# A joint pool for retention and the second MLP, with own raw places for attention's later weights and the first MLP's adaLN and up tiles

## The chip, the cores and the metric

The kernel runs on one core of a Trainium2 chip. The metric is the device time of one execution in microseconds (us); three executions of the kernel before took 1850.36, 1853.43 and 1853.51 us, and their median, 1853.43, is the time before.

## The reference

Two layers over 512 latent tokens of width 1024, with 256 context tokens beside them. Layer 0 mixes by neighbourhood attention (8 heads) and spatial gating, layer 1 by bidirectional retention (8 heads); each mixer is followed by a gated MLP with a depthwise convolution of width 3 over the tokens. Shift, scale and gate of every block (adaLN) come from a product of a conditioning vector with `ada_w`. Cut to what matters:

```python
for i in range(2):
    mod_lat = silu(c) @ ada_w[i] + ada_b[i]      # six parts: shift, scale, gate, twice
    mod_ctx = silu(c_ctx) @ ada_w[i] + ada_b[i]
    h = modulate(rmsnorm(x, g[i, 0]), sh1, sc1)  # the same for the context
    y = hybrid(h_ctx, h) if i == 0 else retention(h_ctx, h)
    x = x + g1 * rmsnorm(y, g[i, 1])
    h = modulate(rmsnorm(x, g[i, 2]), sh2, sc2)
    x = x + g2 * rmsnorm(conv_ffn(h), g[i, 3])   # context too, in layer 0 only

def conv_ffn(h):                                 # 1024 -> 2 x 2816 -> 1024
    gate, up = split(dwconv3(h @ w_in, conv_w, conv_b), 2)
    return (silu(gate) * up) @ w_out
```

## The kernel before, in words

`Trunk.build` runs five stages one after the other: spatial gating (`sgu`), attention, the first MLP (`ffn`, l = 0, 768 tokens in 770 columns), retention, and the second MLP (`ffn`, l = 1, 512 tokens). Every instruction is issued through `Lane.call` (line 63), so all rows of the profile name that line, and tiles tell them apart. Buffers come from pools: a tile asked for under a tag takes the tag's next place and waits until the readers of the tile that was there are done. A scheduler sets the order in which each engine's instructions stand; once set, each engine works through its row in order. SP issues the loads, and waits in front of a load for its place to be free; POOL (GpSimd) issues the sums in DRAM that collect the MLP's output.

A weight tile of 128 x 1024 (512 KB) is loaded into a raw place, and `split` (line 99) turns it into a high part, copied by ACT, and a low part, subtracted by DVE. A product of two such pairs takes three matmuls (`mm3`, line 142). Raw places are three under the tag "raw" in the pool "bp", and nearly all loads share them: attention's weights, adaLN tiles, the MLP's weights.

Attention (line 883) goes through four pairs of heads with ten steps each. `project_pair` (line 970) loads and splits a pair's q, k and v weights (tiles wq2r, wq2h, wq2l for the third pair's q, and so on) and makes the projections pq, pk, px, py; at step 9 it is called for the pair two on.

The MLP (line 1794) runs over 22 columns j of the hidden width. For each, `weights(j)` loads a gate tile (f0010r is column 10's in the first MLP) and an up tile (f0110r), and makes from them and their sums seven half-size weights (wa, wb, wc, wd with s and q) for a product scheme with seven products in place of eight (px, py, pz). ACT and DVE gather the products in `pre`, `conv` makes the convolution, the silu and the product (cv, g), and every second column the pieces of the output product (wf) with w_out's tiles (fo09r is column 9's) follow; ACT copies them to yp or ypg, and POOL adds them to yd in DRAM. The up tile has a place of its own ("rawu"), the gate and output tiles share "raw". The first two columns are made without the scheme by `plain`: pf from the first tokens' halves (hb), pf100b and its like from the second half of the tokens (b), with weights wp1 (loaded ahead by `early`), wp01, wp10 and wp11. b comes out of the residual of the stage before: yr, xd and the transposes ht of each token tile, then sa or sb and the block sums.

Beside the first MLP run jobs of adaLN (`ada_half`, line 259): six halves of four tiles each (ar), each tile multiplied and added on DVE in four products (acc), taken in turns that `bg` gives at set places of the loop. Beside attention and retention run jobs that use PE (`ada_packed`).

Retention and the second MLP each have a pool of their own. A pool opened where another was closed takes its memory, so the second MLP opens with placeholder tiles that order its places.

## Time and profile before

| | us |
|---|---|
| median of the three runs | 1853.43 |
| the profiled execution | 1849.05 |
| its span, first to last instruction | 1847.3 |
| PE busy | 1771.2 |
| DVE busy | 1411.9 |
| ACT busy | 1134.7 |
| POOL busy | 314.3 |
| mean granted TensorE clock | 0.987 of full |

PE (TensorE) is the matmul engine, DVE (VectorE) and ACT (ScalarE) the elementwise ones, SP the queue that issues loads. In the profile's rows `out<-in` names the tiles, `x` a count. A row of a timeline gives the start, the duration, the engine, and in brackets the idle time of the engine before the instruction with what ended it. A row of the waits gives who waited for whom, the total, the times and the longest. A row of the windows gives each engine's busy time in that stretch, then PE's granted clock (1.00 is full), the mean share of the 16 DMA engines and GB/s.

By the tiles in the trace attention takes from about 108 to 375, the first MLP from 380 to 905, retention to 1465 and the second MLP to the end.

### The profile page before, as it was taken

Reading aid. Unit: us, or ns where it says so; the run is one execution under the profiler, and the core shown is the slowest. Engines: PE = TensorE matmul, PEld = TensorE weight load, DVE = VectorE, ACT = ScalarE, POOL = GpSimd, SP = SyncE. Lnnn points to the kernel's source line nnn. Section 1 sums busy time; section 2 is a strip of 40 time slices with the busy share of each in tenths; the row PEclk is TensorE's granted clock in tenths of the full one; section 3 lists DMA queues with packets and bytes.
Section 4 is the critical chain, followed back from the end, with each engine's and each line's share of the span. In section 5 each row is a group of like instructions: output and inputs, shape, how many; then the busy total and the mean of one; then the engine's idle time right before and its main releaser. Section 6 shows DMA issues by size and latency. Waiting matters only on the chain. (4 is left out here: it accounts for less than half of the span.)

```text
span 1847.3 us, 29784 instructions
## 1 busy us (share of the span) xinstructions
PE 1771.2 (96%) x11240; PEld 1581.0 (86%) x11240; DVE 1411.9 (76%) x2389; ACT 1134.7 (61%) x2078; POOL 314.3 (17%) x453
## 2 busy tenths in 40 slices
PE   6999999999999899999889999999999899899998
PEld 4887777789989799998789989999998789899996
DVE  4544567579797778778787798888899699888887
ACT  4534567556555465564586677667677476666763
POOL 1111211110223122221110001111110201122221
PEclk9999999999999999999999999999999989999999
DMA  8433332324687778677657434666643235677773
GB/s 310 137 106 97 110 109 70 125 71 148 160 187 151 162 147 178 138 168 158 231 186 224 132 126 128 172 168 166 171 116 122 97 116 148 173 194 175 191 175 103
DMA packets 95488, 279.21 MB, mean 151 GB/s; under 512 B 12528, under 2 KB 14064, under 8 KB 95344
## 3 DMA queue, kind: packets, MB, share of 16 engines
q1 hardware_dynamic: 63568, 217.88, 36.4%
q0 software_dynamic: 31200, 59.31, 19.1%
q8 instruction: 88, 1.44, 0.3%
q14 instruction: 56, 0.46, 0.1%
q10 hardware_dynamic: 576, 0.11, 0.0%
HBM read 208.06 MB, written 52.43 MB: 141 GB/s over the span
## 5 line engine op out<-in xcount | busy, mean ns | idle before, releaser
L63 DVE SCALAR_TENSOR_TENSOR cv<-pre,cw,cv 128x769 f32<-128x769 f32 (+1 forms) x176 | 152.8, 880 | 8.0 <-ACT cv L63 7.4
L63 ACT ACTIVATE cv<-pre,cw 128x770 f32<-128x770 f32 (+1 forms) x88 | 81.0, 922 | 39.7 <-DVE pre L63 38.5
L63 DVE SCALAR_TENSOR_TENSOR acc<-ar,cs,acc 128x512 f32<-128x512 f32 x112 | 81.7, 746 | 26.6 <-DMA ar<-in_adaw 17.2
L63 POOL DMA_DIRECT2D yf<-yp x64 | 55.8, 872 | 260.8 <-ACT yp L63 241.9
L63 ACT ACTIVATE pre<-px 128x256 f32<-128x256 f32 (+2 forms) x160 | 54.2, 366 | 41.4 <-PE px L63 40.5
L63 POOL DMA_DIRECT2D yd<-yp x54 | 46.6, 871 | 191.9 <-ACT yp L63 188.0
L63 ACT COPY yp<-wf 128x512 f32<-128x512 f32 x118 | 67.8, 576 | 17.9 <-PE wf L63 17.7
L63 POOL DMA_DIRECT2D yd<-ypg x54 | 45.3, 864 | 154.3 <-ACT ypg L63 153.8
L63 POOL DMA_DIRECT2D yr<-ryp x40 | 32.7, 828 | 136.6 <-ACT ryp L63 125.3
L63 ACT ACTIVATE g<-cv 128x770 fp32r<-128x770 f32 (+1 forms) x44 | 32.4, 737 | 27.8 <-DVE cv L63 27.7
L63 ACT ACTIVATE pre<-py 128x384 f32<-128x384 f32 (+1 forms) x40 | 17.4, 435 | 46.3 <-DVE cv L63 25.5
L63 PE MATMUL px<-hs,wd 128*128 128x384 f32 x240 | 45.3, 336 | 0.1
L63 PEld LDWEIGHTS px<-hs,wd 128*128 128x128 f32 x240 | 42.3, 188 | 2.0 <-DVE pre L63 0.5
L63 ACT ACTIVATE cv<-cv 128x770 f32<-128x770 f32 (+1 forms) x44 | 32.7, 743 | 14.7 <-DVE cv L63 14.4
L63 DVE TENSOR_TENSOR g<-cv,g 128x770 fp32r<-128x770 f32 (+1 forms) x44 | 36.1, 821 | 7.0 <-ACT g L63 6.7
L63 DVE TENSOR_TENSOR pre<-pre,pz 128x256 f32<-128x256 f32 (+1 forms) x60 | 20.9, 371 | 26.4 <-PE pz L63 26.4
L63 PE MATMUL ad<-ar,c 128*32 128x512 f32 (+1 forms) x320 | 39.4, 529 | 0.1
L63 ACT ACTIVATE sc<-sc,sst 128x512 f32<-128x512 f32 x32 | 23.2, 726 | 24.0 <-DVE sc L63 21.9
L63 DVE TENSOR_TENSOR cv<-cv 128x770 f32<-128x770 f32 (+1 forms) x44 | 36.1, 821 | 1.0
L63 POOL TENSOR_TENSOR tm<-slab,mask 128x256 f32<-128x256 f32 (+1 forms) x32 | 25.6, 828 | 65.9 <-DVE sst L63 65.7
L63 DVE CUSTOM_DVE_ANT_0 sc<-s,tm 128x256 f32<-128x256 f32 x32 | 13.5, 420 | 30.4 <-PE s L63 22.8
L63 PEld LDWEIGHTS px<-hs 128*128 128x128 f32 x240 | 31.4, 193 | 5.9 <-DVE pre L63 4.7
(2998 smaller groups left out, 6876.7 us busy)
## 6 DMA issues: line engine op xcount, KB each, us to landing
ar<-in_adaw SPq DMA_DIRECT2D x96, 512.0 KB, 4.3
yf<-yp POOLq DMA_DIRECT2D x64, 256.0 KB, 4.5
yd<-yp POOLq DMA_DIRECT2D x54, 256.0 KB, 5.2
yd<-ypg POOLq DMA_DIRECT2D x54, 256.0 KB, 4.6
yr<-ryp POOLq DMA_DIRECT2D x40, 256.0 KB, 4.4
fin<-xd SPq DMA_DIRECT2D x10, 512.0 KB, 4.1
xd<-xd SPq DMA_DIRECT2D x8, 512.0 KB, 3.1
xn<-in_x SPq DMA_DIRECT2D x6, 512.0 KB, 4.6
```

Of the source, the lines that this page charges most:

```text
L63: r = f(*p, **k)
```

## The change

Three things are done. In attention the q, k and v weights of the third and fourth pair are loaded into a tile of three raw places (`raws3`, tag "sa"); the third pair's loads are asked for ahead of the loop, the fourth's as each place is read, and the splits stand at steps 4, 6 and 8 of the pair two before, in place of its step 9. In the first MLP a tile `ars` of three places under "sa" holds two adaLN tiles, each loaded one unit before its use, and a spare place that takes the up tile of every odd column from 3; the shared places are left to gate and output weights. Each of these jobs gets one more turn at its start, and columns above 15 one more turn each. And retention and the second MLP share a pool ("rfp"), in which the second MLP's tiles take over tags of retention's; `early(1)` also loads and splits wp01 and wp10 during retention's end. In `plain` the second column's convolution comes after the rest of the block sums.

The diff, with `...` where lines are left out:

```diff
     def phase(self, ctx, name, extra):
-        self.xp = ctx.enter_context(self.tc.tile_pool(name=name, bufs=1))
+        self.xp = self.joint or ctx.enter_context(self.tc.tile_pool(name=name, bufs=1))
...
+    def ada_ring(self, n, items):
...
+        t = self.bp.tile([P, n, 1024], F32, name=f"ars{items[0][0]}{items[0][1]}", tag="sa", bufs=1)
+        self.ars = [t[:, i] for i in range(n - 1)]
+        self.spare = t[:, n - 1]
+        self.units = [(l, half, kp) for l, half in items for kp in range(4)]
+        self.unit_n = 0
+        for x, u in zip(self.ars, self.units):
+            self.load(x, self.ada_unit_src(*u))
...
+    def ada_raw(self):
...
+        i, n = self.unit_n, len(self.ars)
+        self.unit_n += 1
+        if i and i - 1 + n < len(self.units):
+            self.load(self.ars[(i - 1) % n], self.ada_unit_src(*self.units[i - 1 + n]))
+        return self.ars[i % n]
...
     def ada_half(self, l, half, streams, gate=None, away=False, fine=False):
...
+        if l == 0 or half < 4:
+            yield
...
-            raw = self.bp.tile([P, 1024], F32, name=f"ar{l}{half}{kp}", tag="raw", bufs=3)
-            self.load(raw, self.ada_unit_src(l, half, kp))
+            if l == 0 or half < 4:
+                raw = self.ada_raw()
+            else:
+                raw = self.bp.tile([P, 1024], F32, name=f"ar{l}{half}{kp}", tag="raw", bufs=3)
+                self.load(raw, self.ada_unit_src(l, half, kp))
...
-            self.b12 = [
-                [self.xp.tile([P, 2, n], F32R, name=f"b12{l}{x}{m}", tag=f"g{x}", bufs=4 if l else 3) for m in range(2)]
-                for x in range(2)
-            ]
+            if l:
+                both = [self.xp.tile([P, 2, 2, n], F32R, name=f"b12{l}{x}", tag=f"gt{x}", bufs=1) for x in range(2)]
+                self.b12 = [[b[:, m] for m in range(2)] for b in both]
+            else:
+                self.b12 = [
+                    [self.xp.tile([P, 2, n], F32R, name=f"b12{l}{x}{m}", tag=f"g{x}", bufs=3) for m in range(2)]
+                    for x in range(2)
+                ]
...
+            self.raws3 = self.bp.tile([P, 3, 1024], F32, name="raws3", tag="sa", bufs=1)
+            raws = [self.pair_raw(2, k) for k in range(3)]
...
+                if i < n and step in (4,6,8) and j < 2:
+                    k = (4,6,8).index(step)
+                    pairs[j + 2].setdefault("w", []).append(self.pair_unit(j + 2, k, raws.pop(0)))
+                    if j == 0:
+                        raws.append(self.pair_raw(3, k))
...
+    def pair_raw(self, j, i):
+        raw = self.raws3[:, i]
+        self.load(raw, self.a["hyb_qkv"][(4 * i + j) * P : (4 * i + j + 1) * P])
+        return raw
...
+    def pair_unit(self, j, i, raw=None):
+        if raw is None:
+            return self.unit(self.a["hyb_qkv"][(4 * i + j) * P : (4 * i + j + 1) * P], f"w{'qkv'[i]}{j}")
+        hi, lo = self.slot(f"w{'qkv'[i]}{j}")
+        self.split(hi, lo, raw)
+        return hi, lo
...
     def project_pair(self, j, pr):
...
-        w = [self.unit(self.a["hyb_qkv"][(4 * i + j) * P : (4 * i + j + 1) * P], f"w{'qkv'[i]}{j}") for i in range(3)]
+        w = pr["w"] if "w" in pr else [self.pair_unit(j, i) for i in range(3)]
...
         def lat(i):
...
-            cos = rp.tile([P, 512], F32, name="cos", tag="cos")
-            sin = rp.tile([P, 512], F32, name="sin", tag="sin")
+            turns = rp.tile([P, 2, 512], F32, name="turns", tag="turns")
+            cos, sin = turns[:, 0], turns[:, 1]
+            tb = rp.tile([P, 2, 2, 4, 256], F32R, name="rtb", tag="blk")
...
-                self.blk["t", i] = rp.tile([P, 2, 4, 256], F32R, name=f"rt{i}b", tag=f"t{i}")
+                self.blk["t", i] = tb[:, i // 2]
...
             def context(h):
...
-                d["sc"] = rp.tile([P, 2, 256], F32, name=f"cs{h}", tag="cs", bufs=1)
+                d["sc"] = rp.tile([P, 2, 256], F32, name=f"cs{h}", tag="acc0", bufs=1)
...
-            cw = fp.tile([P, 44, 4], F32, name=f"cw{l}", tag="cw")
+            cw = fp.tile([P, 44, 4], F32, name=f"cw{l}", tag="cw" if first else "e0")
...
-            if not first:
-                for tag in ("rawu", "wh5", "wl5", "wh6", "wl6", "pre0", "pre1"):
-                    fp.tile([P, 1024], F32R if tag[0] == "w" else F32, name=f"at{tag}", tag=tag, bufs=1)
...
-            pres = [fp.tile([P, 2, W], F32, name=f"pre{l}{i}", tag=f"pre{i}") for i in range(1 if first else 2)]
+            pres = [fp.tile([P, 2, W], F32, name=f"pre{l}{i}", tag=("pre", "st")[l] + str(i)) for i in range(1 if first else 2)]
...
-            else:
-                for tag in ("cv", "wh4", "wl4"):
-                    fp.tile([P, 1024], F32R if tag[0] == "w" else F32, name=f"at{tag}", tag=tag, bufs=1)
-            ng = 3 if first else 4
+            ng = 3
+            held = {}
...
-                "o": ("y0", "y4", "y2") if first else ("w2", "w5", "w6"),
+                "o": ("y0", "y4", "y2") if first else ("w2", "w6", "w5"),
...
             def slot(kind, name):
...
+                if h == "w6":
+                    return [fp.tile([P, 1024], F32R, name=f"{name}{x}", tag=f"rv{m}", bufs=1) for m, x in enumerate("hl")]
...
             def raw(src, name, up=False):
-                if up:
-                    t = fp.tile([P, 1024], F32, name=f"{name}r", tag="rawu", bufs=1)
+                if up and first and up % 2 == 0 and up > 3:
+                    t = self.spare
+                elif up:
+                    t = fp.tile([P, 1024], F32, name=f"{name}r", tag="rawu" if first else "rg", bufs=1)
...
             def win(j, i):
...
-                return raw(a["ffn_in"][r : r + P], f"f{l}{i}{j}", i == 1)
+                return raw(a["ffn_in"][r : r + P], f"f{l}{i}{j}", i and j + 1)
...
             def conv(j, pre):
-                cv = fp.tile([P, 2, W], F32, name=f"cv{l}{j}", tag="cv", bufs=1)
+                cv = fp.tile([P, 2, W], F32, name=f"cv{l}{j}", tag="cv" if first else "of", bufs=1)
...
+                elif not first:
+                    i = j % 4
+                    if i == 1 and not held:
+                        held["g"] = self.bp.tile([P, 4, 512], F32R, name="gsa", tag="sa", bufs=1)
+                    if i in (1, 2):
+                        g = held["g"][:, 2 * i - 2 : 2 * i]
+                    else:
+                        g = fp.tile([P, 2, 512], F32R, name=f"g{l}{j}", tag="turns" if i == 0 else "gt0", bufs=1)
+                    g = [g[:, 0], g[:, 1]]
...
-                        if (j, i) == (js[0], 0):
-                            u = self.wp
-                            ring["i" if first else "o"] += 1
+                        if (j, i) in self.wps:
+                            u = self.wps[j, i]
+                            if first:
+                                ring["i"] += 1
...
-                            if (j, i) == (js[1], 1):
-                                ring["i"] = 3
-                            u = slot("i" if (j, i) == (js[1], 1) else "o", f"wp{i}{j}")
-                        if u is not self.wp:
+                            ring["o"] = 2
+                            u = slot("o", f"wp{i}{j}")
+                        if (j, i) not in self.wps:
...
+                    if j != js[0]:
+                        steps[1 + j]()
+                        for _ in sums:
+                            pass
...
-                    steps[1 + j]()
-                for _ in sums:
-                    pass
+                    if j == js[0]:
+                        steps[1 + j]()
...
             def w_out(f, kind="o"):
...
             def part():
...
-                    tiles = [fp.tile([P, 2 if first else 4, 512], F32, name=f"yp{l}", tag="yp")]
-                    if first:
+                    tiles = [fp.tile([P, 2, 512], F32, name=f"yp{l}", tag="yp")]
+                    if not first:
+                        tiles.append(fp.tile([P, 2, 512], F32, name="ypt", tag="gt1", bufs=1))
+                    else:
...
+            if first:
+                self.ada_ring(3, [(0, 10), (0, 11), (1, 0), (1, 1), (1, 2), (1, 3)])
...
+                if first and j > 15:
+                    self.bg()
...
-        self.lp = None
+        self.lp = self.joint = None
...
+            self.wps = {(0, 0): self.wp}
+            if l:
+                for j, i, tags in ((0, 1, ("rv0", "rv1")), (1, 0, ("wh4", "wl4"))):
+                    if i:
+                        raw = self.xp.tile([P, 1024], F32, name=f"wp{j}{i}r", tag="rg", bufs=1)
+                    else:
+                        raw = self.bp.tile([P, 1024], F32, name=f"wp{j}{i}r", tag="raw", bufs=3)
+                    r = (44 * l + NF * i + j) * P
+                    self.load(raw, a["ffn_in"][r : r + P])
+                    self.wps[j, i] = [self.xp.tile([P, 1024], F32R, name=f"wp{j}{i}{x}", tag=g, bufs=1) for x, g in zip("hl", tags)]
+                    self.split(*self.wps[j, i], raw)
...
+        with ExitStack() as ctx:
+            self.joint = ctx.enter_context(self.tc.tile_pool(name="rfp", bufs=1))
...
```

24 lines of the change are left out of this document (12 added, 12 removed).

## The prediction

> **What bounds the kernel now.** I read the page's engine shares first, then what PE waits for, then windows, then the timelines of four places. PE is the bound; what a change can win is PE's idle time and the time at a lowered clock.
>
> ```profile
> PE 1771.2 (96%) x11240; PEld 1581.0 (86%) x11240; DVE 1411.9 (76%) x2389; ACT 1134.7 (61%) x2078; POOL 314.3 (17%) x453
> PE wf L63 <- ACT ypg L63: 6.5, 2, 4.6
> PE ht L63 <- DVE sb L63: 4.9, 3, 4.1
> PE px L63 <- ACT pre L63: 3.9, 2, 3.1
> PE pf100b L63 <- ACT b L63: 2.8, 1, 2.8
> PE at L63 <- ACT arow L63: 2.0, 1, 2.0
> PE wf L63 <- ACT yp L63: 1.5, 2, 1.3
> PE pq L63 <- ACT wq2h L63: 1.5, 1, 1.5
> PE pq L63 <- DVE wq2l L63: 1.3, 1, 1.3
> ```
>
> PE idles 1847.3 - 1771.2 = 76.1 us. The waits (total, times, longest) are few and long, and ACT or DVE is named as releaser; the question is what those were waiting for. The windows (after PE, PEld, DVE, ACT and POOL come the granted clock, the DMA share and GB/s) show what a gap costs beyond itself:
>
> ```profile
> 188.00:198.00 10.00, 6.87 (x25) 5.40 (x26) 7.90 (x17) 8.13 (x19) 5.87 (x7) 0.66 0.51 161
> 600.00:610.00 10.00, 9.71 (x51) 8.77 (x49) 7.91 (x14) 3.06 (x6) 1.23 (x2) 1.00 1.01 225
> 610.00:620.00 10.00, 5.70 (x23) 5.12 (x24) 7.24 (x11) 5.46 (x11) 2.64 (x3) 0.83 0.46 81
> 650.00:700.00 50.00, 50.00 (x263) 45.84 (x262) 41.25 (x61) 28.99 (x50) 13.29 (x17) 1.00 0.76 153
> 880.00:890.00 10.00, 6.93 (x33) 6.62 (x32) 7.96 (x11) 6.05 (x13) 0.00 (x0) 0.83 0.40 141
> 1470.00:1480.00 10.00, 5.89 (x42) 5.47 (x42) 6.62 (x12) 5.67 (x15) 3.18 (x5) 0.87 0.15 57
> 1480.00:1490.00 10.00, 6.91 (x39) 6.18 (x38) 9.15 (x15) 7.43 (x14) 0.59 (x1) 0.61 0.51 151
> 1500.00:1550.00 50.00, 49.96 (x363) 46.93 (x362) 49.06 (x79) 37.29 (x67) 0.31 (x1) 1.00 0.34 111
> ```
>
> If the clock is either whole or half, a mean of 0.66 over 10 us is 10 x 0.34 / 0.5 = 6.8 us at half speed; each busy one of them loses half a microsecond. From 650 to 700, in the first MLP, PE lost nothing: the steady state is PE's, and the losses lie in single places.
>
> **Part 1, attention.** The third pair's weights: SP, ACT, PE and DVE in turn.
>
> ```profile
> 180.86 0.33 SPq L63 DMA_DIRECT2D ar<-in_adaw  x1
> 181.28 0.38 SPq L63 DMA_DIRECT2D wq2r<-in_hyb_qkv  x1
> 189.45 1.04 ACT L63 ACTIVATE wq2h<-wq2r 128x1024 fp32r<-128x1024 f32 x1
> 190.55 0.74 PE L63 MATMUL pq<-h0a,wq2h 128*128 128x512 f32 x1 [1.50 <-ACT wq2h L63]
> 192.20 1.21 DVE L63 TENSOR_TENSOR wq2l<-wq2r,wq2h 128x1024 fp32r<-128x1024 f32 x1
> 193.46 0.79 PE L63 MATMUL pq<-h0a,wq2l 128*128 128x512 f32 x1 [1.31 <-DVE wq2l L63]
> ```
>
> The load stands behind an adaLN load in SP's row, and its high and low parts are split only when PE wants them. SP's row here, before:
>
> ```order
> L63 DMA slab_2209<-in_rpb 128x1x256
> L63 DMA ar_1858<-in_adaw 128x1024
> L63 DMA wq2r<-in_hyb_qkv 128x1024
> L63 DMA wk2r<-in_hyb_qkv 128x1024
> L63 DMA wv2r<-in_hyb_qkv 128x1024
> ```
>
> and now (raws is the new place of three tiles; pair 2's loads stand far ahead, these are pair 3's):
>
> ```order
> L63 DMA raws_1208<-in_hyb_qkv 128x1024
> L63 DMA ar_1868<-in_adaw 128x1024
> L63 DMA slab_2214<-in_rpb 128x1x256
> L63 DMA raws_1208<-in_hyb_qkv 128x1024 x2
> L63 DMA ar_1872<-in_adaw 128x1024
> ```
>
> No q, k or v load competes for the three shared places any more, and the splits come at steps 4, 6 and 8. That removes 1.50 + 1.31 = 2.8 us, and the slow clock: of 6.8 us at half speed 1.31 is the second gap itself, so (6.8 - 1.3) / 2 = 2.7 us. Sum **5.5**. The splits (1.04 on ACT, 1.21 on DVE, three times each) are moved, not added, into a stage where both have room (8.13 and 7.90 of 10 even in the worst window). Bounds: 2.7, if something else keeps the clock down, to 5.5. The Trainium skill, "TensorE: Matmul & The Clock Gate", section "What's actually happening", has the clock fall after an idle window of about 3.4 us. Here it fell with no gap above 1.50, so the trace disagrees; by the page part 1 would be worth 2.8 and the sum 2.7 us less, 1835.3.
>
> **Part 2, first MLP.** The longest gap, in SP, DVE, ACT and PE, then the two late ones:
>
> ```profile
> 605.13 0.33 SPq L63 DMA_DIRECT2D ar<-in_adaw  x1
> 606.27 0.33 SPq L63 DMA_DIRECT2D fo09r<-in_ffn_out  x1
> 611.44 0.75 DVE L63 SCALAR_TENSOR_TENSOR acc<-ar,cs,acc 128x512 f32<-128x512 f32 x1 [3.53 <-DMA ar<-in_adaw]
> 612.75 1.03 ACT L63 ACTIVATE cv<-pre,cw 128x770 f32<-128x770 f32 x1 [6.91 <-DVE pre L63]
> 614.30 0.80 PE L63 MATMUL wf<-fo06h,g 128*128 128x512 f32 x1 [4.59 <-ACT ypg L63]
> 850.39 0.75 DVE L63 SCALAR_TENSOR_TENSOR acc<-ar,cs,acc 128x512 f32<-128x512 f32 x1 [2.80 <-DMA ar<-in_adaw]
> 878.03 1.06 ACT L63 ACTIVATE fo019h<-fo019r 128x1024 fp32r<-128x1024 f32 x1 [2.78 <-DMA fo019r<-in_ffn_out]
> ```
>
> An adaLN tile is issued at 605.13 and used at 611.44, 6.3 us later; DVE stands 3.53 us in front of it, the conv's input behind it holds ACT for 6.91, and the ypg copies queued behind that hold PE for 4.59. SP before, around this place:
>
> ```order
> L63 DMA ar_5850<-in_adaw 128x1024
> L63 DMA f0011r<-in_ffn_in 128x1024
> L63 DMA ar_5951<-in_adaw 128x1024
> L63 DMA fo09r<-in_ffn_out 128x1024
> L63 DMA ar_6102<-in_adaw 128x1024
> L63 DMA f0111r<-in_ffn_in 128x1024
> ```
>
> and now (ars is the ring of two adaLN places and the spare one, which takes every second up tile):
>
> ```order
> L63 DMA ars_4179<-in_adaw 128x1024 x2
> L63 DMA f0010r<-in_ffn_in 128x1024
> L63 DMA f0110r<-in_ffn_in 128x1024
> L63 DMA fo08r<-in_ffn_out 128x1024
> L63 DMA f0011r<-in_ffn_in 128x1024
> L63 DMA fo09r<-in_ffn_out 128x1024
> L63 DMA ars_4179<-in_ffn_in 128x1024
> ```
>
> The adaLN load runs a unit ahead (of four products each), and gate and output weights keep the three shared places. What can go: 4.59, 1.97 (arow, behind the 850.39 product), 3.06 (px, behind fo019h) and 1.29 (yp) = 10.9, and half of 3.4 us of slow clock in each of the windows 610 and 880, 1.7 + 1.7: together 14.3. The fo019 and yp gaps wait for output weights, which gain only by freer places; I take half of 3.1 + 1.3 + 1.7 = 6.1 off, so 14.3 - 3.0 = **11.3**; bounds 4 (only the first gap, less its clock) and 14.3. Six further turns of the background job are nothing beside a PE that is full; the same number of products runs either way.
>
> **Part 3, retention into the second MLP.** PE, DVE and SP here:
>
> ```profile
> 1472.80 0.28 PE L63 MATMUL pf<-hb,wp1h 128*128 128x256 f32 x1
> 1474.35 0.28 PE L63 MATMUL pf<-hb,wp1l 128*128 128x256 f32 x1
> 1478.74 1.97 PE L63 MATMUL ht<-ident,yr 128*128 128x128 f32 x8 [4.11 <-DVE sb L63]
> 1483.46 0.55 PE L63 MATMUL pf100b<-b,wp1h 128*128 128x256 f32 x1 [2.75 <-ACT b L63]
> 1477.87 0.49 DVE L63 TENSOR_SCALAR yr<-xd,xd3r 128x512 f32<-128x512 f32 x1 [1.19 <-POOL xd3r L63]
> 1482.18 1.22 DVE L63 TENSOR_TENSOR wp01l<-f101r,wp01h 128x1024 fp32r<-128x1024 f32 x1 [0.34 <-DMA acc<-in_adab_row]
> 1476.07 0.32 SPq L63 DMA_DIRECT2D xd<-xd  x1
> 1479.13 0.42 SPq L63 DMA_DIRECT2D f110r<-in_ffn_in  x1
> ```
>
> The last tile's chain (xd3r on POOL, yr on DVE) frees the transposes at 1478.74, and PE has nothing else, because the next weights load after the last xd store. PE's row before:
>
> ```order
> L63 MATMUL pf_15170<-hb_14872,wp1l 128x256
> L63 MATMUL ht_15245<-ident,yr_14708 128x128 x4
> L63 MATMUL ht_15254<-ident,yr_14708 128x128 x4
> L63 MATMUL pf100b<-b_15263,wp1h 128x256
> L63 MATMUL pf101b<-b_15263,wp01h 128x256
> ```
>
> and now, from the end of the blocks for wp01 and wp10 (24 products each, moved here):
>
> ```order
> L63 MATMUL pf_15166<-hb_14844,wp10l 128x256
> L63 MATMUL pf_15166<-hb_14844,wp10h 128x256 x2
> L63 MATMUL pf_15166<-hb_14844,wp10l 128x256
> L63 MATMUL ht_15191<-ident,yr_14668 128x128 x4
> L63 MATMUL ht_15200<-ident,yr_14668 128x128 x4
> L63 MATMUL pf_15219<-hb_14844,wp11h 128x256 x2
> ```
>
> Between 1472.80 and 1474.35 thirteen such products start: 0.119 us each. 48 take 5.7 us and cover the 4.11 gap, the transposes starting 1.6 later; 24 of wp11 behind them take 2.9 and cover the 2.75. The clock: 10 x (0.13 + 0.39) / 0.5 = 10.4 us at half, some 4.0 of them idle (1.2 before 1478.74, 2.75), so 6.4 / 2 = 3.2. PE gets 4.1 + 2.75 + 3.2 = 10.0 us ahead. But from 1500 to 1550 DVE is busy 49.06 of 50; it feeds PE's weights, and itself gains only two splits moved forward into its idle time, 2 x 1.22, a third partly, and the microsecond it idles there: 2.4 to 5, I take 5 less 1 for wp01's split (1.04 and 1.22), which now stands in ACT's and DVE's rows within the first tile's residual chain: **4**; bounds 2 - 2.3 (nothing kept, the splits all on the chain) and 10.0. In SP's row cw, fo10r, wp01r and f111r now stand ahead of the xd stores; wp01r waits for the last rg transposes and f111r for wp01's split, both ahead of the first store's data, so I cost that at nothing beyond the microsecond above. Merging the pools adds and removes no instruction. It moves one load at the start of retention:
>
> ```profile
> 890.95 0.33 SPq L63 DMA_DIRECT2D rcv00r<-in_ret_vg  x1
> 898.32 0.33 SPq L63 DMA_DIRECT2D rcv01r<-in_ret_vg  x1
> ```
>
> rcv00r now waits behind the nine fin loads that stood between these two, at most 898.32 - 890.95 = 7.4 us later. The row after it already lives with such a start, so I cost it at nothing; a context value product that had to wait for all of it would cost up to those 7.4.
>
> **Sum.** 1849.05 (the profiled execution; span 1847.3) - 5.5 - 11.3 - 4 = 1828.2. That execution lies 4.4 under the median 1853.43, so 1853.4 - 20.8 = **1832.6**.
>
> **Rivals.**
> - *DVE keeps all of part 3* (12%): it is 98% busy where PE gets ahead; part 3 gives nothing, 1836.6. Against: DVE idles 0.34 to 1.19 at a time ahead of 1483.
> - *The loads stay late in the first MLP* (14%): the window 600 to 610 shows a DMA share of 1.01, so a load issued earlier meets the output accumulations of POOL; part 2 gives 3, 1840.9. Against: 0.76 in the steady stretch where PE is full. The Trainium skill ("DMA: Bandwidth & Descriptors", "Issuing engines are not separate DMA queues") says that loads of all queues share the same engines, which speaks for this rival; the 1.01 agrees.
> - *SP's row holds gate loads back* (9%), slower: an ars load waits in SP for the products of the unit before, and f0010r or f0012r stand behind it. With 22 such loads, more than 20.8 / 22 = 0.95 us lost at each eats all gains; at 1.5 each, half of the 3.06 behind fo019h, it is 33 - 20.8 = 12 slower, 1865. For: PE gaps behind late fo loads. Against: 650 to 700 has the same loads in the same queue without loss.
> - *It doesn't do what it says* (5%): if the places of one tile are waited for as a whole, or the same gaps come elsewhere, 1853, no difference.
>
> **Numbers.** The forecast has 60%. All gains at their upper bounds are 5.5 + 14.3 + 10.0 = 29.8, 1823.6; at their lower ends 2.7 + 4 + 0 = 6.7, 1846.7. The range 1822 to 1846 holds the forecast and the first two rivals. Faster by over 0.2% (3.7 us, about what a measurement here can tell from none): 0.60 + 0.12 + 0.14 = 0.86; within: 0.05; slower: 0.09.
>
> **Right or wrong.** Right: no PE wait for wq2 and a clock near 1 from 188 on; no DVE idle on adaLN tiles in the first MLP and no 4.59 gap; ht waits under 1 us at the start of the second MLP, with DVE full after it. Wrong: PE waits on wa or fo weights in the first MLP (the SP rival), or on wc and fo splits around 1490 to 1520 that sum to 10 us (the DVE rival).

## The result and the profile after

| | before | changed |
|---|---|---|
| median of four runs, us | 1851.89 | 1834.84 |
| lowest to highest, us | 1848.15 to 1853.51 | 1830.70 to 1836.59 |
| ratio, changed to before | | 0.9918 [0.9891, 0.9944] |
| the profiled execution, us | 1849.05 | 1836.59 |
| its span, us | 1847.3 | 1834.8 |

The changed kernel is faster by 0.82%: 1851.89 x (1 - 0.9918) = 15.2 us, and by the ends of the interval 10.4 to 20.2. The forecast was 1832.6, with 20.8 saved. The profiled execution of the changed kernel is the slowest of its four, so it shows 12.5 of the gain. Two executions below, one of only_mlp1 and one of only_joint, ran at a mean granted clock of 0.845 and 0.890 (1931.92 and 1893.92 us) and are in no ratio, and the profiled execution of ngr_act ran at 0.952 and is in no comparison of stages.

The page's engine shares and the waits of PE in the changed kernel that the argument turns on (who waits for whom, total, times, longest):

```profile
PE 1768.0 (96%) x11240; PEld 1577.6 (86%) x11240; DVE 1410.8 (77%) x2389; ACT 1141.8 (62%) x2084; POOL 315.4 (17%) x453
PE ht L63 <- DVE xn L63: 11.7, 4, 9.3
PE px L63 <- DVE pre L63: 5.0, 4, 1.6
PE wf L63 <- DVE fo05l L63: 3.1, 1, 3.1
PE ht L63 <- DVE yr L63: 3.0, 1, 3.0
PE wf L63 <- ACT ypg L63: 2.6, 2, 2.1
PE s L63 <- POOL kb L63: 2.6, 1, 2.6
PE rx L63 <- DVE of L63: 2.4, 1, 2.4
PE ht L63 <- DVE sb L63: 0.8, 2, 0.4
```

All eight waits shown of before are gone or cut: pq on wq2h and wq2l, pf100b on b, at on arow and wf on yp have no row any more, wf on ypg fell from 6.5 to 2.6, ht on sb from 4.9 to 0.8, px on ACT's pre from 3.9 to 2.3 (shown with tap_after below). But other waits stand there now: s on kb, ht on yr and wf on fo05l, 2.6 to 3.1 us each, and rx on of, which is 2.4 in this execution, 0.65 to 1.76 in the other kernels with the joint pool and 0.91 in the kernel before. The largest of all, ht on xn, lies at the start of the program (11.3 before) and none of the parts bears on it; the next, px on DVE's pre (3.4 before), lies for the most part in the second MLP (3.0 of 5.0). The windows of the changed kernel, laid where the work of the windows shown before now is (the stages start 3 to 15 us earlier), and three more, at 145, 520 and 530:

```profile
145.00:155.00 10.00, 7.41 (x29) 5.87 (x28) 2.62 (x7) 3.42 (x5) 2.00 (x3) 0.83 0.52 193
188.00:198.00 10.00, 9.97 (x59) 6.76 (x59) 6.14 (x20) 7.45 (x21) 4.49 (x6) 1.00 0.49 148
520.00:530.00 10.00, 8.62 (x46) 7.83 (x45) 6.89 (x12) 6.03 (x9) 0.86 (x1) 1.00 0.77 178
530.00:540.00 10.00, 8.32 (x35) 7.39 (x36) 9.97 (x15) 5.70 (x10) 1.72 (x3) 0.83 0.72 158
610.00:620.00 10.00, 10.00 (x45) 8.98 (x44) 10.00 (x15) 5.56 (x12) 3.73 (x5) 0.85 0.96 254
870.00:880.00 10.00, 10.00 (x59) 9.92 (x58) 9.86 (x15) 6.12 (x10) 0.00 (x0) 1.00 0.14 52
1459.00:1469.00 10.00, 10.00 (x79) 9.58 (x78) 8.19 (x13) 6.89 (x16) 2.96 (x4) 1.00 0.31 106
1469.00:1479.00 10.00, 10.00 (x85) 9.79 (x84) 9.18 (x18) 8.22 (x19) 0.00 (x0) 1.00 0.00 0
1489.00:1539.00 50.00, 46.90 (x315) 41.60 (x315) 47.65 (x75) 33.05 (x59) 1.83 (x2) 1.00 0.37 114
```

The window at 188 went from 0.66 of the clock to 1.00, the ones at the joint of retention and second MLP from 5.89 and 6.91 of 10 to full, the one at 880 (now 870) from 6.93 to full. The one at 610 went from 5.70 to full, but its clock is still 0.85 behind a gap of 2.06 that ends at 609.49. The losses moved: 145 to 155 (before, PE was 9.92 busy there at a clock of 1.00), 520 to 540, and the first 50 us of steady work in the second MLP, where PE went from 49.96 to 46.90.

Three rows of PE stand in every kernel here and cut the span into four stages: the first product with the second tokens' b in the first MLP, the first Ykq of retention, and the first kn behind a gap. In the kernel before:

```profile
391.35 0.44 PE L63 MATMUL pf000b<-b,wp0h 128*128 128x384 f32 x1 [1.76 <-ACT b L63]
1081.27 0.50 PE L63 MATMUL Ykq<-h1c,rkq21h 128*128 128x256 f32 x2 [0.95 <-ACT qp L63]
1402.59 1.08 PE L63 MATMUL kn<-ident,kp 128*128 128x128 f32 x4 [2.41 <-DVE kp L63]
```

and in the changed one:

```profile
388.02 0.69 PE L63 MATMUL pf000b<-b,wp0h 128*128 128x384 f32 x1 [1.76 <-ACT b L63]
1066.72 0.50 PE L63 MATMUL Ykq<-h1c,rkq21h 128*128 128x256 f32 x2 [0.96 <-ACT qp L63]
1388.10 1.09 PE L63 MATMUL kn<-ident,kp 128*128 128x128 f32 x4 [2.41 <-DVE kp L63]
```

Stage A (to the first row, with attention) is 391.4 before and 388.0 after; stage B (first MLP and retention's start) 689.9 and 678.7; stage C 321.3 and 321.4; stage D (retention's end and second MLP) 444.7 and 446.7. So in this pair of executions attention gave 3.4, the first MLP 11.2, and the joint with the second MLP took 2.0. Single executions of the same code differ in A and D by 5 to 6 us, as the table of all kernels below shows, so it takes more of them to say what each part gave.

### The profile page after: what moved, and what is told of

Read it like the earlier page. It is cut to its first block, busy times and chain, and to the rows that moved or that the text cites. A ratio compares the mean times of both kernels' runs of the same rounds, so it can differ in the third digit from the quotient of the medians.

```text
span 1834.8 us, 29748 instructions
## 1 busy us (share of the span) xinstructions
PE 1768.0 (96%) x11240; PEld 1577.6 (86%) x11240; DVE 1410.8 (77%) x2389; ACT 1141.8 (62%) x2084; POOL 315.4 (17%) x453
## 3 DMA queue, kind: packets, MB, share of 16 engines
q0 software_dynamic: 31200, 59.31, 19.1%
## 5 line engine op out<-in xcount | busy, mean ns | idle before, releaser
L63 DVE SCALAR_TENSOR_TENSOR acc<-ars,cs,acc 128x512 f32<-128x512 f32 x96 | 70.1, 749 | 19.1 <-DMA acc<-in_adab_row 9.8
L63 ACT COPY yp<-wf 128x512 f32<-128x512 f32 x86 | 49.5, 577 | 13.1 <-PE wf L63 13.1
L63 POOL DMA_DIRECT2D yf<-yp x32 | 28.0, 876 | 160.7 <-ACT yp L63 96.0
L63 POOL DMA_DIRECT2D yf<-ypt x32 | 27.9, 873 | 100.1 <-ACT ypt L63 74.1
L63 PE MATMUL px<-hs 128*128 128x256 f32 x240 | 32.6, 285 | 5.3 <-DVE pre L63 5.0
```

The source lines that it names most:

```text
L63: r = f(*p, **k)
```

## The experiments

The theory after the result was that the three parts add up, each in its own stage, and that what was given back has three places: a bias load in attention, the adaLN places in the first MLP, and DVE behind the joint. The rivals were that a part only works together with another, and that one of the three gives nothing or costs time. Every kernel was timed in five rounds against the kernel before on the same chip.

| kernel | us | before on that chip | ratio |
|---|---|---|---|
| only_att | 1842.24 | 1850.62 | 0.9949 [0.9931, 0.9967] |
| only_mlp1 | 1844.41 | 1850.62 | 0.9964 [0.9948, 0.9981] |
| only_joint | 1848.92 | 1850.62 | 0.9979 [0.9963, 0.9995] |
| again (the changed kernel) | 1833.34 | 1850.62 | 0.9897 [0.9879, 0.9916] |
| ring3 | 1839.15 | 1848.22 | 0.9948 [0.9929, 0.9967] |
| nospare | 1849.74 | 1848.22 | 1.0006 [0.9989, 1.0022] |
| late_split | 1833.34 | 1848.22 | 0.9913 [0.9895, 0.9932] |
| slab2 | 1832.85 | 1848.22 | 0.9922 [0.9900, 0.9944] |
| spare_only | 1840.25 | 1848.19 | 0.9951 [0.9933, 0.9970] |
| wp01_out | 1832.93 | 1848.19 | 0.9907 [0.9879, 0.9936] |
| tap_after | 1821.55 | 1848.19 | 0.9847 [0.9821, 0.9873] |
| ngr_act | 1832.68 | 1848.19 | 0.9917 [0.9887, 0.9946] |

The stages of the profiled executions, and the two new gaps of PE: the one in front of the score product that reads kb (attention) and the one in front of fo05l (first MLP).

| kernel | A | B | C | D | gap kb | gap fo05l |
|---|---|---|---|---|---|---|
| before | 391.4 | 689.9 | 321.3 | 444.7 | none | 0.37 |
| changed | 388.0 | 678.7 | 321.4 | 446.7 | 2.59 | 3.06 |
| again | 387.4 | 681.2 | 321.3 | 443.8 | 2.61 | 3.89 |
| only_att | 385.9 | 685.1 | 321.3 | 448.9 | 1.16 | 0.31 |
| only_mlp1 | 392.0 | 682.9 | 321.4 | 446.3 | 0.89 | 6.55 |
| only_joint | 392.0 | 690.6 | 321.9 | 442.5 | none | none |
| ring3 | 386.2 | 688.1 | 321.4 | 442.4 | 1.47 | 4.29 |
| nospare | 385.1 | 698.7 | 321.2 | 444.3 | 1.91 | 4.31 |
| late_split | 383.0 | 679.1 | 321.5 | 448.0 | none | 3.35 |
| slab2 | 383.2 | 678.8 | 321.4 | 442.1 | none | 3.35 |
| spare_only | 384.9 | 689.1 | 321.6 | 444.8 | 1.85 | 5.91 |
| wp01_out | 386.7 | 682.0 | 321.2 | 442.2 | 1.82 | 4.45 |
| tap_after | 384.7 | 679.9 | 321.4 | 433.7 | 1.12 | 2.56 |

The stages of ngr_act are left out for its clock.

### The parts one by one

**only_att**: the kernel before with the attention part alone. The core of the edit:

```diff
+            self.raws3 = self.bp.tile([P, 3, 1024], F32, name="raws3", tag="sa", bufs=1)
+            raws = [self.pair_raw(2, k) for k in range(3)]
...
+                if i < n and step in (4,6,8) and j < 2:
+                    k = (4,6,8).index(step)
+                    pairs[j + 2].setdefault("w", []).append(self.pair_unit(j + 2, k, raws.pop(0)))
```

> The kernel before with the attention part alone. My theory (each part gives its own share of the sum, 5.5 + 11.3 + 4): 5.5 us faster, no PE wait for wq2 and a full clock around 190. The rival read from the changed kernel's trace (a wait of PE for kb, behind a bias slab's load of 6 us in SP's row, takes the place of the wq2 waits): 3 us faster or less, with a PE gap of some 2.6 us near 145 and 3.4 us at half clock behind it.

Measured: 0.9949 [0.9931, 0.9967], 9.4 us (6.1 to 12.8).

**only_mlp1**: the kernel before with the ring of two adaLN places, the spare up place and the further turns alone.

```diff
+            if first:
+                self.ada_ring(3, [(0, 10), (0, 11), (1, 0), (1, 1), (1, 2), (1, 3)])
...
+                if first and j > 15:
+                    self.bg()
```

> The kernel before with the first MLP's part alone (adaLN ring, spare up place, more turns). My theory: 11.3 us faster, the 4.59 gap gone. The rival (loads still meet the output accumulations): DVE still idles 3 us on an adaLN tile once or twice, 9 us faster. The rival of SP's row, held-back gate loads: slower, or under 4 us faster.

Measured: 0.9964 [0.9948, 0.9981], 6.6 us (3.5 to 9.6).

**only_joint**: the kernel before with the joint pool, wp01 and wp10 early, and the order of `plain` alone (the order in both MLPs).

```diff
+                for j, i, tags in ((0, 1, ("rv0", "rv1")), (1, 0, ("wh4", "wl4"))):
...
+                    self.split(*self.wps[j, i], raw)
```

> The kernel before with the joint pool alone (early wp01 and wp10, the second column's convolution after the block sums in both MLPs). My theory: 4 us faster, the gaps of 4.11 and 2.75 gone. The rival (wp01's split in the residual chain and DVE in the second MLP give the gain back, as the changed kernel's profile has it): no difference or up to 2 us slower, with a gap of about 3 us in front of the second tile's ht transposes and 4 to 6 us more of small PE gaps from 1490 to 1750.

Measured: 0.9979 [0.9963, 0.9995], 3.9 us (0.9 to 6.8).

**again**: the changed kernel, no edit.

> The changed kernel once more, on the same chip as its three parts. If the parts are independent, its difference is the sum of theirs within 3 us (my theory: 20.8, measured first 17). If a part only works with another, the sum is off by more than that.

Measured: 0.9897 [0.9879, 0.9916], 19.1 us (15.5 to 22.4). The product of the three parts is 0.9949 x 0.9964 x 0.9979 = 0.9892, 20.0 us. So within the intervals the parts add up, no part costs time, and none of them needs another.

The stages say the same with other weights. A is 391.8 in the mean of the three kernels without part 1 and 385.8 in the nine that have it and one place for the bias slab (slab2 has two): -6.0. B is 688.5 without part 2 (before, only_att, only_joint) and 680.4 with all of it (seven kernels): -8.1. D is 446.6 without part 3 (before, only_att, only_mlp1) and 444.3 with it (the eight that leave no work out): -2.3, with a spread of 442 to 448. Together 16.4. Between parts 1 and 2 the two ways differ by 3.4 and 1.5, and that is as far as it is settled: only_att's stage B is 4.8 shorter than before's and its D 4.2 longer, though the edit touches neither, so a stage of one execution is good to some 4 or 5 us. One source of that spread is the clock: the executions called changed, again and late_split (whose edit changed nothing, see below) are of one program, and in D, ahead of the last product, the clock fell to half 3, 1 and 4 times for 3.41 us each, up to 1.7 us of work lost each time, and D took 446.7, 443.8 and 448.0.

### The first MLP: which of its two places works

**ring3**: the changed kernel with a third adaLN place in the place of the spare up place.

```diff
-        self.ars = [t[:, i] for i in range(n - 1)]
+        self.ars = [t[:, i] for i in range(n)]
...
-                if up and first and up % 2 == 0 and up > 3:
-                    t = self.spare
-                elif up:
+                if up:
```

> The changed kernel with three adaLN places in the ring and the up tiles back in their single place (the spare is the third). Theory from the last runs (in the changed kernel a load of the ring can start only when the unit before last is read, and where DVE's row has units close together that is some 5 us ahead, as long as a load takes): no DVE wait on ars in the first MLP, the gap of 3 to 6.5 us in front of fo05l's product gone, 2 to 5 us faster than the changed kernel, some 22 under before. Rival (the spare place for the up tiles gives the gain): the adaLN wait goes, but gaps behind up tiles come back, 3 us or more slower than the changed kernel.

Measured: 0.9948 [0.9929, 0.9967]; stage B 688.1. It is slower than the changed kernel, as the rival had it; DVE's waits on adaLN tiles fell to 3.4 and did not go.

**nospare**: the changed kernel without the spare up place and with two adaLN places.

```diff
-                if up and first and up % 2 == 0 and up > 3:
-                    t = self.spare
-                elif up:
+                if up:
```

> The changed kernel with the ring of two adaLN places, and the up tiles back in their single place. If the spare is worth nothing: as the changed kernel, 17 to 19 under before. If the spare carries part 2: 3 us or more slower than the changed kernel, with PE waits on wb or wd behind an up load.

Measured: 1.0006 [0.9989, 1.0022]; stage B 698.7. It loses not 3 us but all of the gain.

**spare_only**: the changed kernel with the spare up place, but with the adaLN tiles back in the three shared places.

```diff
-                raw = self.ada_raw()
...
+            raw = self.bp.tile([P, 1024], F32, name=f"ar{l}{half}{kp}", tag="raw", bufs=3)
+            self.load(raw, self.ada_unit_src(l, half, kp))
```

> The changed kernel with the adaLN tiles back in the three shared places, each loaded when its turn comes; the spare place for every second up tile and the additional turns stay. Theory from the last runs (the spare place carries part 2; the ring's loads are late too where the second stream's accumulator starts late): as the changed kernel, 17 to 19 under before, with DVE waits on adaLN tiles of about 17 in all again. My first theory (the adaLN ring carries part 2): 5 or more slower than the changed kernel.

Measured: 0.9951 [0.9933, 0.9970]; stage B 689.1. The theory that the spare place carries part 2 fell. Parts 1 and 3 alone would make 0.9949 x 0.9979 = 0.9928, and ring3 and spare_only stand at 0.9948 and 0.9951: neither place gains anything by itself, and B goes back to the 688.5 of kernels without part 2. Only both together take it to 680.4. With neither spare nor third adaLN place (nospare) B is 10 longer than without part 2: the ring then costs time. Between the MLP's last product and the first Ykq, where the scheduler set another order for PE, it takes 147.5, against 144.9 in the mean of the three without part 2; the other 7.6 lie in the MLP itself. Why is open. Nor do these kernels differ from the changed one by a place alone: the scheduler gave DVE's row another order in each of them, from 418 on in ring3 and nospare and from 489 on in spare_only.

What DVE waits for in the first MLP shows the one half of the reason. In the kernel before (window 385 to 905), in the changed kernel (380 to 895), and in spare_only (380 to 895):

```profile
DVE pre L63 <- PE pz L63: 15.7, 8, 5.0
DVE acc L63 <- DMA ar<-in_adaw: 12.9, 6, 3.5
```

```profile
DVE pre L63 <- PE pz L63: 40.2, 10, 6.7
DVE acc L63 <- DMA ars<-in_adaw: 9.0, 3, 4.0
```

```profile
DVE acc L63 <- DMA ar<-in_adaw: 19.6, 8, 6.4
```

The ring halves the adaLN waits beside the shared places (9.0 against 19.6 with the same jobs and turns), but it doesn't end them: three remain, up to 4.0. The spare up place shows in the other row: with it DVE stands 40.2 in front of PE's pz (38.6 in spare_only), without it 15.7 before, 13.7 in ring3 and 16.8 in nospare. So with the spare place DVE runs further ahead of PE. What the ring adds shows in PE's rows. Without the adaLN ring the wait of px on pre comes back in spare_only, where the kernel before had 3.06 of it:

```profile
876.95 1.01 PE L63 MATMUL px<-hs,wc21h 128*128 128x384 f32 x2 [3.05 <-ACT pre L63]
```

### The new gap at fo05l

In every kernel with the further turns of the jobs PE waits 2.6 to 6.6 us for the low part of an output weight, which took 0.37 before. In the changed kernel SP, DVE and PE have:

```profile
512.16 0.33 SPq L63 DMA_DIRECT2D f018r<-in_ffn_in  x1
520.78 2.38 SPq L63 DMA_DIRECT2D ars<-in_adaw  x2
```

```profile
525.88 1.42 DVE L63 SCALAR_TENSOR_TENSOR acc<-ars,cs,acc 128x512 f32<-128x512 f32 x2 [3.07 <-DMA ars<-in_adaw]
530.41 1.22 DVE L63 TENSOR_TENSOR fo05l<-fo05r,fo05h 128x1024 fp32r<-128x1024 f32 x1
531.68 0.80 PE L63 MATMUL wf<-fo05l,g 128*128 128x512 f32 x1 [3.06 <-DVE fo05l L63]
```

SP's loads stand still from 512.16 to 520.78, then two adaLN tiles are issued within 2.4, DVE needs the first at 525.88, 5.1 later, and waits 3.07 for it with the split of fo05l behind. PE waits the same 3.06. The weight itself had landed: PE was using fo05h from 528.22 on, so this is DVE's row and no load of an output weight.

The adaLN load is asked for late: SP issues it when DVE has read the place before (520.77), and with the further turns DVE is ready for the next unit 2 us after that, at 522.8; in the kernel before, the load issued at 521.16 was first read at 528.21. Why the place comes free late was followed in the order of the rows: the second stream's accumulator of this half is filled behind the half before's norm rows, for which DVE waits 1.96 (510.84) and 1.26 (514.92), and both streams read each tile. And the load is slow: over its 5.1 us the DMA share is 0.95, which the mean of 0.77 over 520 to 530 hides, and from 520 to 527 the queue that POOL's output sums go by took the larger part of the DMA engines' time, that of the loads 40.0%:

```profile
q0 software_dynamic: 311, 0.57, 57.7%
```

In the other kernels with this gap the tile took from 4.5 us (late_split, gap 3.35) to 7.9 (only_mlp1, gap 6.55) from its issue to DVE's use. Spare_only, which has no ring, has the gap too (5.91, the tile 7.0 after its issue). So the ring neither makes it nor takes it away.

**ngr_act** puts the loads of these norm rows on ACT's queue, where POOL issued them, and gives the bias slab two places (as slab2 does).

```diff
-                G.dma_start(ngr, self.a["norm_g"][row : row + 1, h * 512 : h * 512 + 512].broadcast_to([P, 512]))
+                (S if away else G).dma_start(
+                    ngr, self.a["norm_g"][row : row + 1, h * 512 : h * 512 + 512].broadcast_to([P, 512])
+                )
```

> The changed kernel with two bias slab places, and with the norm weights' row for the first MLP's gate loaded from ACT's queue, not POOL's, where it stands behind accumulations. Theory: DVE's wait for that row (2.6) shrinks below 1, the second stream's accumulator starts earlier, the ring's loads go out earlier, and the gap in front of fo05l's product (3 to 6.5) falls under 2 with its half clock gone; with the slab's 2.6 + 1.7 gone too, 5 to 9 us faster than the changed kernel, 1825 to 1829. Rival (the load is late because of the shared DMA engines): the gap of 3 or more stays; 0 to 4 faster.

Measured: 0.9917 [0.9887, 0.9946]; the gap at fo05l was still 2.70, as the rival had it. The first steps of the theory came about: DVE's wait for the second norm row is gone (that for the first is 2.51), the second stream's first product stands at 513.81 (517.27 in the changed kernel), and the adaLN load goes out at 518.32 (520.78). But DVE has the tile only at 524.93, 1.0 earlier: it took 6.6 us in place of 5.1, at a DMA share of 1.02 (and with PE at 0.95 of its clock). Nor did a third adaLN place close the gap (ring3: 4.29). So its immediate cause is shown by the rows, DVE held by an adaLN tile that lands late; late issue and slow load both have a part in it, and no run separates them.

### Attention: the bias slab

**slab2**: the changed kernel with two places for the bias slab of attention.

```diff
-        slab = ap.tile([P, 256], F32, name=f"slab{h}", tag="slab", bufs=1)
+        slab = ap.tile([P, 256], F32, name=f"slab{h}", tag="slab", bufs=2)
```

> The changed kernel with two places for the bias slab instead of one. Theory (the slab load, which waits for POOL to be done with the slab before and then takes 6 us, holds kb and with it PE at 145): the gap of 2.6 there is gone and the clock full, 2.6 + 1.7 = 4.3 us faster than the changed kernel. Rival (kb waits in POOL's row for something else): no difference.

Measured: 0.9922 [0.9900, 0.9944]; stage A 383.2, no gap at kb. In the kernel before, POOL and PE have here:

```profile
145.65 0.40 POOL L63 TENSOR_SCALAR slab<-slab 128x256 f32<-128x256 f32 x1 [4.63 <-DMA slab<-in_rpb]
146.12 1.59 POOL L63 CAST kb<-kb 64x768 fp32r<-64x768 f32 x2
146.99 0.39 PE L63 MATMUL s<-kb,q 128*128 128x256 f32 x1
```

in the changed kernel SP, POOL and PE:

```profile
140.74 0.62 SPq L63 DMA_DIRECT2D slab<-in_rpb  x1
146.78 0.41 POOL L63 TENSOR_SCALAR slab<-slab 128x256 f32<-128x256 f32 x1 [6.07 <-DMA slab<-in_rpb]
148.13 0.39 PE L63 MATMUL s<-kb,q 128*128 128x256 f32 x1 [2.59 <-POOL kb L63]
```

and in slab2 the window that was at 7.41 and 0.83:

```profile
145.00:155.00 10.00, 10.00 (x64) 8.08 (x62) 5.04 (x15) 6.07 (x11) 0.83 (x1) 1.00 0.51 178
```

POOL stands in front of the slab, whose load waits for its one place, the casts of kb stand behind that on POOL, and PE takes kb as soon as the first cast is done. In the kernel before that was just in time: PE came to kb at 146.9. In the changed kernel PE comes there at 145.53, 1.4 earlier, and the slab took 1.4 longer to land. So the gap is a wait that had no slack before; it shows when PE is ahead, and in only_mlp1, whose attention is as before, it shows with 0.89. A second place takes it away: A is 383.2 (and 383.0 in late_split, where the load took 4.5 us and there was no gap either), against 384.7 to 388.0 where the gap was 1.12 to 2.61. Of the eight executions of part 1 with the gap only three show a fall of the clock behind it (changed, again and wp01_out, A 386.7 to 388.0); the other five have A 384.7 to 386.2. In the whole kernel's time these 2 to 5 us don't show: 0.9922 against 0.9918 and 0.9897 for the changed kernel, within each other's intervals.

### The joint: what was given back

**late_split**: the changed kernel with wp01's split written in `plain`, behind the residual, its load still early.

```diff
+                            if not first and i:
+                                self.split(*u, self.wpr)
...
-                    self.split(*self.wps[j, i], raw)
+                    if i:
+                        self.wpr = raw
```

> The changed kernel with wp01 loaded ahead but split only in the second MLP's first part, after the residual chain. My theory (the split of 1.05 on ACT and 1.22 on DVE stands in the first tile's residual chain): the gap of 2.9 in front of the second tile's ht transposes is 1.5 again, as before, and no half clock follows it; 1 to 3 us faster unless PE then waits for wp01. Rival (the load itself, or DVE's order, makes the gap): it stays 2.9.

Measured: 0.9913 [0.9895, 0.9932]. The edit did nothing: the scheduler put wp01h and wp01l at the same place of ACT's and DVE's rows, in the first tile's residual chain. So it tells nothing on the split and is one more run of the changed program: PE, DVE, ACT and POOL have the same instructions in the same order.

**wp01_out**: wp01's load and split are left out and its products take wp1's tiles.

```diff
-                for j, i, tags in ((0, 1, ("rv0", "rv1")), (1, 0, ("wh4", "wl4"))):
+                self.wps[0, 1] = self.wp
+                for j, i, tags in ((1, 0, ("wh4", "wl4")),):
```

> The changed kernel without wp01's load and split: its products take wp1's tiles instead, the same number of matmuls. My theory (the split stands in the residual chain): the gap in front of the second tile's ht transposes falls from 2.9 to 1.5, the half clock behind it goes, and the chain from gt7l to the second tile's yr takes 15.2 again instead of 17.0; 1 to 3 us faster than the changed kernel. Rival (PE's row, with the transposes moved ahead of two products, makes the gap): it stays near 2.9.

Measured: 0.9907 [0.9879, 0.9936]; stage D 442.2. The changed kernel, on DVE, POOL and PE:

```profile
1437.43 1.22 DVE L63 TENSOR_TENSOR wp01l<-wp01r,wp01h 128x1024 fp32r<-128x1024 f32 x1
1437.63 1.72 POOL L63 TENSOR_SCALAR wyd<-ssyd 128x1 f32<-128x1 f32 x1 [12.59 <-ACT jyd L63]
1449.89 1.54 PE L63 MATMUL ht<-ident,yr 128*128 128x128 f32 x6 [2.95 <-DVE yr L63]
```

and wp01_out:

```profile
1435.58 0.30 POOL L63 TENSOR_SCALAR wyd<-ssyd 128x1 f32<-128x1 f32 x1 [11.07 <-ACT jyd L63]
1446.63 0.98 PE L63 MATMUL ht<-ident,yr 128*128 128x128 f32 x7 [1.45 <-DVE yr L63]
```

With the split the chain from the last low part of the products' input (gt7l) to the second tile's yr takes 1432.33 to 1449.35, 17.0 us; without it 1430.92 to 1446.09, 15.2, which is also what it takes in the kernel before (1443.79 to 1458.96). So the split costs 1.8 in the chain and the 1.5 by which the gap in front of ht grew (1.45 to 2.95). Behind the longer gap the clock is at half for 3.4 us (0.83 in the window 1449 to 1459), 1.7 more; in wp01_out it isn't, but neither is it in the repeat, which has the same gap (2.94). Of the 1.8, 1.4 lie in a step of POOL that took 1.72 in place of 0.30 and overlaps with DVE's making of wp01l; it took 1.71 or 1.72 in all nine kernels with that split there and 0.30 in the three without. In the whole time these 1.5 to 3.2 don't show.

**tap_after**: the changed kernel without one tap of the convolution (w2's product and sum on DVE) in the second MLP.

```diff
-                    V.scalar_tensor_tensor(
-                        out=d[:, 0 : W - 1], in0=s[:, 1:W], scalar=w2, in1=d[:, 0 : W - 1], op0=ALU.mult, op1=ALU.add
-                    )
+                    if first:
+                        V.scalar_tensor_tensor(
+                            out=d[:, 0 : W - 1], in0=s[:, 1:W], scalar=w2, in1=d[:, 0 : W - 1], op0=ALU.mult, op1=ALU.add
+                        )
```

> The changed kernel with one of the convolution's two DVE products left out in the second MLP (the tap of the next token), which takes some 0.6 us a piece and 44 pieces from DVE there. If DVE bounds PE from 1490 on (my theory): the PE gaps behind DVE between 1490 and 1660, 11 to 12 us in the changed kernel, fall under 4, and the kernel is 6 to 10 us faster than the changed one. Rival (late loads make these gaps): they stay above 8, and it is at most 3 faster.

Measured: 0.9847 [0.9821, 0.9873]; stage D 433.7 against 444.3. PE's waits in the second MLP, in the changed kernel from 1485 to 1640:

```profile
PE px L63 <- DVE pre L63: 3.0, 2, 1.6
PE px L63 <- ACT pre L63: 2.3, 2, 1.2
PE px L63 <- DVE wa3l L63: 1.5, 1, 1.5
PE wf L63 <- DVE fo17l L63: 1.0, 1, 1.0
PE wf L63 <- DVE fo13l L63: 0.8, 1, 0.8
PE wf L63 <- DVE fo11l L63: 0.6, 1, 0.6
```

in tap_after from 1480 to 1635:

```profile
PE px L63 <- DVE pre L63: 3.4, 1, 3.4
PE px L63 <- ACT pre L63: 0.4, 1, 0.4
PE wf L63 <- DVE fo11l L63: 0.2, 1, 0.2
```

and in the kernel before from 1490 to 1650:

```profile
PE px L63 <- DVE pre L63: 2.8, 2, 2.6
PE wf L63 <- DVE fo15l L63: 1.3, 1, 1.3
PE px L63 <- ACT pre L63: 0.9, 1, 0.9
```

They sum to 9.2, 4.0 and 5.0. So PE starts the steady part earlier and waits 4.2 more for DVE and ACT in it; with less to do on DVE these waits fall by 5.2 and the stage is 10.6 shorter. DVE's load sets a part of this stage. How much of the 10.6 the kernel before would gain by the same edit wasn't tried.

One row more splits stage D into what the joint gained and what it gave back: the first px of the second MLP, which has the same number of products ahead of it and behind it in every kernel. From the start of D to that row it is 103.5 us in the mean of the three kernels without part 3 and 95.3 in that of the eight with it, 8.2 less; from there to the end 343.2 and 349.1, 5.9 more, and 340.6 in tap_after.

## Why the prediction was right, and where its sizes were off

**The sum.** Forecast 20.8, measured 15.2 (10.4 to 20.2) and, in the repeat, 19.1 (15.5 to 22.4). The sign and the mechanism of each part held; two of the three terms were mis-sized, in opposite directions by the ratios (9.4 for 5.5, 6.6 for 11.3). That the sum came out as near as it did is in part luck.

**Part 1 (term 5.5): right, with a wait it didn't name.** The gaps at wq2 and the slow clock from 188 on are gone, as named. It measured 6.0 by stage A and 9.4 (6.1 to 12.8) by the ratio, all of which lies above the term's upper bound of 5.5; what the ratio has beyond stage A isn't found in any row. The Trainium skill's rule in "TensorE: Matmul & The Clock Gate", section "What's actually happening", by which the slow clock there would not have come from the two short gaps, made it 2.8; the window 188 to 198 at 1.00 without those gaps decides for the trace. What the part gave back is the gap at kb: the step missed is to ask, of the wait that is next on PE's path, how much slack it had. The rows of before show none (kb cast from 146.12, taken at 146.99).

**Part 2 (term 11.3): mechanism right, mis-sized, 6.6 by the ratio and 8.1 by stage B.** The step that failed is "the adaLN load runs a unit ahead": in most turns it does, but at three of the five changes from one half to the next (waits at 526, 791 and 859) it doesn't: at the first of them the two places are released 2.1 us apart and the first load is due by then, so DVE still stands 9.0 in front of adaLN tiles (12.9 before) and the sign "no DVE idle on adaLN tiles" was wrong. That costs the gap at fo05l, 3.06, and the 3.4 at half clock behind it in this execution (0.83 over 10 us is 10 x 0.17 / 0.5), 1.7: 4.8 together. Of the 4.59 gap 2.06 stayed, and the half clock behind it too (from 609.67, 3.4 us), 1.7: 3.8 that the term had counted as gone. The 14.3 of its upper bound less 4.8 and 3.8 is 5.7, near the 6.6 by the ratio. What it removed outright are the gaps of 3.06 (px), 1.97 and 1.29 and the slow clock at 880. The doubt about the output weights, for which 3.0 was taken off, was unneeded, since their gap closed; that it stood in for a part of the 8.6 that came back elsewhere was luck. And the term gave all of the credit to the adaLN places, while ring3 shows that the spare up place is needed as much.

**Part 3 (term 4): right within what can be measured, 3.9 (0.9 to 6.8) by the ratio, 2.3 by stage D.** PE got its full windows (4.11 and 2.75 both closed and the clock at 1.00) and came to the first px 8.2 us earlier, where the forecast had 10.0 ahead of the split; 5.9 of that were given back behind it, 4.2 of them as waits for DVE and ACT. Two signs were wrong in size: ht waits 2.95 and not under 1, since the split in the chain was costed as 1 and costs 1.5 there, with the clock up to 3.2; and the waits on wc and fo splits, named for the rival at 10, sum to 9.2 of all kinds, of which 5.0 stood there before.

**The rivals.** "The loads stay late in the first MLP" is half true: an adaLN load is late, by the order of releases and also by DMA load (a share of 0.95 over its 5.1 us, with POOL's sums as the larger part, against 0.76 in the stretch where PE lost nothing), as this rival had it; but part 2 gave more than the 3 it left (6.6, 3.5 to 9.6). "SP's row holds gate loads back" did not happen in the changed kernel: PE has no wait on a gate weight in the first MLP. Its wait on fo05l is by the letter the sign that was named for this rival, but the weight had landed, and it is DVE's. nospare, which has a wait on a gate weight's split (wa21l, 1.7) and is 10 us longer in B than without part 2, shows that such a loss is near. "DVE keeps all of part 3" fell, narrowly: the part alone is 0.9979 [0.9963, 0.9995], and most of the 8.2 us went back behind it. "It doesn't do what it says" fell with each part's own gain.

## What to carry to other kernels

Where one engine is busy 96% of the time, list its few long waits, find for each the place in memory that the releaser's load was waiting for, and give that load a place of its own; look at what is next on the path and how much slack it has, since a gain of a few microseconds uncovers it. A prefetch ring only runs ahead as long as its places are released in turn: look at the ends of the jobs, where all of them can come free late and close together, and at what else the DMA engines carry just then, over the length of the load and not over a wide window. Try each new place alone, since here two places in one stage gained nothing by themselves and 7 to 8 us together.

## What the runs showed of the hardware that was not expected

PE's clock fell to half behind gaps that are shorter than the 3.41 us for which it then stays there, but not behind every one. In thirteen of the executions (all but ngr_act's) the falls begin whole multiples of 3.413 us apart, in the changed kernel at 148.87, 531.16, 609.67 and 1449.35 among others, and last one, two or three such steps. By the busy times of the traces what decides is how much of one step PE idled: every step with PE idle for more than 0.55 of it was followed by one at half, and from the full clock no fall followed a step idle for less than 0.47. The gap of 3.06 at fo05l lay mostly in one step (PE busy for 0.88 of 3.42), and a fall followed. The gap of 3.35 in late_split lay across two (busy for 1.82 and 1.65 of 3.41 each), and none did. So a gap's length doesn't give its price: the gaps at fo05l, of 2.6 to 6.6, were followed by no fall (late_split, slab2), one step (changed, tap_after) or two (again, only_mlp1, ring3, nospare, wp01_out), which is nothing or up to 1.7 or 3.4 us of work lost.

A step of POOL on 128 x 1 numbers took 0.30 us in wp01_out and 1.72 in the changed kernel, where it overlapped with DVE's subtraction of two 128 x 1024 tiles. The Trainium skill, "GPSIMD Engine Reference", section "1. Specifications", says that POOL shares its interfaces to SBUF with VectorE and contends with VectorE's instructions that have two SBUF inputs; these two rows agree, with a factor of nearly six that the page doesn't give; that the contention is the cause is argued from the overlap and wasn't tried by itself.

The same load at the same place of the program, the bias slab's, took 4.6 us from its issue to POOL's use in the execution before (141.04 to 145.65), 6.0 in the changed kernel's (140.74 to 146.78) and 4.5 in late_split's.
